# Two rows at a time in narrow blocks, a product in halves, and an earlier request for weights, in one layer of a hybrid encoder

## The chip, the cores and the metric

The kernel runs on one core of a Trainium2 chip. Time is the device time of one execution in microseconds (us); smaller is better. Three runs of the kernel before gave 1913.21, 1913.57 and 1913.68 us, so the median is 1913.57. The engines are TensorE (PE; its weight loads are listed apart as PEld), VectorE (DVE), ScalarE (ACT), GpSimd (POOL) and SyncE (SP), which here issues the DMAs.

## The reference

One inference step of a layer with two parallel branches, for 1024 prompt tokens and 32 sample tokens (1056 in all), width 1024, all in float32:

```
h = RMSNorm(x);  z = h @ w_in          # q/k/v of both branches and their gates
o_a = DiffAttn(h)                      # chunk-causal, two softmax maps per head
o_r = Retention(h)                     # per-frame causal, with decay
x = x + (sigmoid(g_a) * o_a + sigmoid(g_r) * o_r) @ w_o
h = RMSNorm(x)
x = x + (silu(h @ w_ff_gate) * (h @ w_ff_up)) @ w_ff_down
x = x + sigmoid(RMSNorm(x) @ w_ple_gate) * (p @ w_ple)
```

It also returns the new keys, values and retention states. The change touches the line with `w_o`, the second RMSNorm, the first of the gate blocks, and the last line.

## The kernel before, in words

Every float32 operand of a large product is split into two float16 parts, high and low, and a product is three matmuls: high by high, high by low, low by high (`mm3`, lines 474 to 476). Tokens lie along the free axis, features across the 128 partitions, so the width 1024 is eight rows k or m of 128 features.

The program has these stages: the heads of both branches (up to about 1054 us); the w_o products; the gate and up products in 22 feature blocks j (from about 1148 us on); the down products; and the last gate with `w_ple_gate`, up to 1912 us.

**w_o.** The 1056 tokens are cut into four blocks c of 352, 352, 176 and 176 tokens (`WIDTH`). A block has eight products m of 24 matmuls. The task `residual(c)` loads the block's old x into a tile `xf` (line 1546, 1.4 MB for a wide block), and for each m multiplies the product's bank by the weight's scale and adds it to its row of `xf` (line 1553, DVE), writes the row out to DRAM (line 1556), squares it on ACT (line 1561) and adds the square to `acc` on DVE (line 1564). After the eighth, four small matmuls `ss` (line 1572) sum `acc` over the partitions, DVE and POOL make the reciprocal root (lines 1576 to 1582), a matmul with `dg` spreads it over the partitions (line 1587), and DVE scales each row of `xf` with it (line 1591).

**Operands of the gate products.** The gate and up products are done by a Strassen-like scheme over two pairs p of blocks: pair 0 is the two wide blocks, pair 1 the two narrow ones. For seven products per pair and feature block it needs, beside the normed rows, sums and differences of rows (`sums`), into the tiles `xh1` (the same memory as `mixs`) and `tT`. Each operand is split into two float16 parts by `parts16`: a copy on ACT (line 1507) and a subtraction. The subtractions, of `parts16` and of `sums`, go through `either_tt` (line 1501), for which a planner picks DVE or POOL.

**Weights of a gate block.** `load_gu(j)` takes one of two stage buffers `st`, issues a 1 MB load on SP (line 1618), squares it on ACT in two halves (line 1630), adds the two sums on DVE (`wamh`, line 1634), lets a matmul `mt` (line 300) sum them over the partitions, makes the scale on DVE (lines 230, 234, 315, 317), and splits the weights and their combinations (lines 1602, 1605 and 1610) into two float16 parts. The stage buffers also hold w_o's weights: `st_16614` those of the third quarter of its columns and `st_16615` those of the fourth, which are split on ACT (line 459) and DVE (line 461).

**What sets the order.** Up to the down products a planner (`Flow`) writes the order of the instructions of PE, DVE, ACT and POOL out by hand. Each task is a generator that yields the estimated cost of its next step on an engine, a buffer to get or put back, or an event. The planner steps through them in estimated time and always takes the step that can start first, then the lower priority number, then the older task. The estimates are in code: a DVE step of n elements, 0.07 + n / 960 us; an ACT step, 0.1 + n / 1200; a POOL step, 0.15 + 0.0021 n; a DMA, 2.9 us for each MB. An engine then takes its instructions strictly in the written order, and waits where an operand is late. SP issues the DMAs in the order of the program. The stage `stream_bc` names the products in order and adds the tasks beside them.

Of the kernel before, what the change touches and what calls it, by code (L numbers as in the profile page):

```python
# [183 lines left out]
def kernel(  # L184
# [1278 lines left out]
    with ExitStack() as pc:  # L1463
# [18 lines left out]
        with ExitStack() as pw:  # L1482
# [18 lines left out]
                ENG[g].tensor_tensor(out=out, in0=in0, in1=in1, op=op)  # L1501


            def parts16(key, out, src):
                CW = WIDTH[2 * key[0]]
                yield S(CW, 0.05)
                nc.scalar.copy(out[0], src)
                yield from either_tt(CW, out[1], src, out[0], ALU.subtract)
                yield ("set", ("o",) + key)

            def sums(c, k):

                p, CW = c // 2, WIDTH[c]
                xa, xf, t = xfs[c - 1], xfs[c], tT[p]
                a1, a3, b2, b4 = xa[:, k], xa[:, HK + k], xf[:, k], xf[:, HK + k]
                cs = span(c)
                yield ("wait", ("o", p, "x1", k))
                yield from either_tt(CW, a1, b2, a1, ALU.subtract)
                flow.add(parts16((p, "t1", k), (xh1[:, k, 0, cs], xh1[:, k, 1, cs]), a1))

                if not p:
                    yield from either_tt(CW, b2, b4, b2, ALU.subtract)
                    flow.add(parts16((p, "x4", k), (xh1[:, HK + k, 0, cs], xh1[:, HK + k, 1, cs]), b4))
                    flow.add(parts16((p, "t3", k), (t[:, T3, k, 0], t[:, T3, k, 1]), b2))
                    yield ("wait", ("o", p, "x4", k))
                    t2 = b4
                else:
                    yield ("wait", ("o", 0, "t2", k))
                    t2 = xfs[0][:, k, 0:CW]
                yield from either_tt(CW, t2, b4, a1, ALU.subtract)  # L1530
                flow.add(parts16((p, "t2", k), (t[:, T2, k, 0], t[:, T2, k, 1]), t2))
                yield ("wait", ("o", p, "x3", k))
                yield from either_tt(CW, a3, t2, a3, ALU.subtract)
                flow.add(parts16((p, "t4", k), (t[:, T4, k, 0], t[:, T4, k, 1]), a3))
                if p:
                    flow.add(parts16((p, "x4", k), (xh1[:, HK + k, 0, cs], xh1[:, HK + k, 1, cs]), b4))
                    yield from either_tt(CW, b2, b4, b2, ALU.subtract)
                    flow.add(parts16((p, "t3", k), (t[:, T3, k, 0], t[:, T3, k, 1]), b2))

            def residual(c):  # L1540

                p, odd = divmod(c, 2)
                CW = WIDTH[c]
                cs = span(c)
                xf = xc.tile([P, KD, CW], F32, tag="xf%d" % p, name="xf", bufs=2)
                nc.sync.dma_start(out=xf, in_=xT[:, :, cs])
                xfs.append(xf)
                yield ("get", "acc")
                acc = wkb.tile([P, CH], F32, tag="acc", name="acc")[:, 0:CW]
                for m in range(KD):  # L1550
                    yield ("wait", ("wo", c, m))
                    yield V(CW, 1.0, 0.08)
                    nc.vector.scalar_tensor_tensor(out=xf[:, m], in0=banks[c, m], scalar=wos[m // 4][1][m % 4 // 2], in1=xf[:, m],
                                                   op0=ALU.mult, op1=ALU.add)
                    yield ("put", "ps")
                    nc.sync.dma_start(out=x1_d[m, :, cs], in_=xf[:, m])
                    if m:
                        yield ("get", "sq")
                    yield S(CW, 0.05)
                    sq = wkb.tile([P, CH], F32, tag="sq", name="sq")[:, 0:CW] if m else acc  # L1560
                    nc.scalar.activation(sq, xf[:, m], AF.Square)
                    if m:
                        yield V(CW)
                        nc.vector.tensor_tensor(out=acc, in0=acc, in1=sq, op=ALU.add)
                        yield ("put", "sq")
                yield ("get", "ss")
                yield ("delay", 2.0 if c + 1 < NW else 0.5)
                yield M(0.3)
                B = CW // 4
                ps = pss.tile([P, 512], F32, tag="ss", name="ss")  # L1570
                for b in range(4):
                    nc.tensor.matmul(out=ps[0:B, CW + b:CW + b + 1], lhsT=acc[:, b * B:(b + 1) * B], rhs=ones32[:, 0:1],
                                     start=True, stop=True)
# [8 lines left out]
                nc.vector.tensor_tensor(out=dg[0:B].rearrange("p (b c) -> p b c", b=4),  # L1582
                                        in0=id32[0:B, 0:B].unsqueeze(1).broadcast_to([B, 4, B]),
                                        in1=r[0:B].unsqueeze(2).broadcast_to([B, 4, B]), op=ALU.mult)
                yield ("delay", 2.0 if c + 1 < NW else 0.5)
                yield M(0.5)
                nc.tensor.matmul(out=ps[:, 0:CW], lhsT=ones32[0:B], rhs=dg[0:B], start=True, stop=True)
                yield ("put", "acc")
                for k in (0, 4, 1, 5, 2, 6, 3, 7):
                    yield V(CW, 1.0, 0.08)  # L1590
                    nc.vector.scalar_tensor_tensor(out=xf[:, k], in0=xf[:, k], scalar=gS[:, 1, k:k + 1], in1=ps[:, 0:CW],
                                                   op0=ALU.mult, op1=ALU.mult)
                    if not odd:
                        flow.add(parts16((p, "x1" if k < HK else "x3", k % HK), (xh1[:, k, 0, cs], xh1[:, k, 1, cs]), xf[:, k]))
# [201 lines left out]
            def stream_bc():  # L1796
# [1 line left out]
                flow.add(residual(0), 0)  # L1798
                flow.add(residual(1), 0)
                for c in range(NW):  # L1800
                    if c == 1:
                        flow.add(load_gu(0), 2)
                        flow.add(load_gu(1), 2)
                    if c == 3:
                        flow.add(load_gu(2), 2)
                    if c in (1, 2):
                        flow.add(residual(c + 1), 0)
                    for m in range(KD):
                        yield ("get", "ps")
# [125 lines left out]
    with ExitStack() as pe:  # L1935
# [3 lines left out]
        for c in range(NCH):  # L1939
# [5 lines left out]
            for m in range(KD):  # L1945
# [1 line left out]
                    norm2(wk, accs[c + 1], xts[c + 1], c + 1)  # L1947
                ms = slice(m % 4 * P, (m % 4 + 1) * P)
                wt = wps[m // 4][0]
                ps = bank()  # L1950
                for k in range(KD):
                    xt = xts[c][k // 4][:, k % 4]
                    mm3(ps, wt[:, k, 0, ms], wt[:, k, 1, ms], xt[:, 0], xt[:, 1], k == 0, k == KD - 1)
                step()
                th = wk.tile([P, CH], F32, tag="th", name="th")
                nc.scalar.activation(th, ps, AF.Tanh, scale=hdp[:, m // 2:m // 2 + 1])
                nc.vector.scalar_tensor_tensor(out=th, in0=th, scalar=1.0, in1=pws[:, m], op0=ALU.add, op1=ALU.mult)
                yo = wk.tile([P, CH], F32, tag="yo", name="yo", bufs=3)
                nc.vector.scalar_tensor_tensor(out=yo, in0=th, scalar=0.5, in1=x2[:, m, cs], op0=ALU.mult, op1=ALU.add)
                nc.sync.dma_start(out=yT[m, :, cs], in_=yo)  # L1960


# [97 lines left out]
```

## Time and profile before

| | before |
|---|---|
| runs, us | 1913.21, 1913.57, 1913.68 (median 1913.57) |
| profiled execution | 1914.65 us, of it the span 1912.8 us |
| PE busy | 1860.5 us (97%) |
| DVE busy | 1503.2 us (79%) |
| ACT busy | 1091.3 us (57%) |
| POOL busy | 681.9 us (36%) |
| mean granted clock of PE | 0.998 |
| w_o products | 1054.4 to about 1145 us |
| DMA | 146.91 MB, mean 77 GB/s |

Busy time is that of the profiled execution. A matmul of 352 columns is listed with 0.31 us, but the next starts 0.15 us behind it, since matmuls overlap; a product's time is read from the starts. A row of the view of waits says for how long an engine stood still for an operand, and who released it. A row in the timeline ends with such a wait in brackets, where there was one.

### The profile page before, as it was taken

To read this page: it belongs to the slowest core of one execution; us is meant where nothing else is said; L and a number is where in the kernel's file an instruction comes from. 1 tells how busy PE (TensorE), PEld (TensorE's weight loads), DVE (VectorE), ACT (ScalarE), POOL (GpSimd) and SP (SyncE) were. 2 spreads that over 40 slices of the span, in tenths; PEclk is the share of its full clock that TensorE was granted. 3 is DMA by queue.
4 is the path that set the end of the run, shared out by engine and by line. 5 is a ranking of instruction groups with operands and counts; after the bars stand their busy time and mean duration, and the time that the engine had idled before them with its cause. 6 is when DMAs were issued, how large, how long until landed. Compare 5 with 4: busy or idle time off the path is not lost.

```text
span 1912.8 us, 38341 instructions
## 1 busy us (share of the span) xinstructions
PE 1860.5 (97%) x14183; PEld 1217.9 (64%) x14183; DVE 1503.2 (79%) x3955; ACT 1091.3 (57%) x2863; POOL 681.9 (36%) x1162
## 2 busy tenths in 40 slices
PE   7899999999999999999999998999999999999999
PEld 3556565555655566555556685777777776666665
DVE  7888888788787787777887589999999986654364
ACT  7777667677676776767656345655555552101132
POOL 3654444445444544544442067232232300000010
PEclk9999999999999999999999999999999999999999
DMA  5122112122021111211215610222111116112031
GB/s 192 71 72 78 60 32 82 36 57 81 26 68 58 50 64 34 80 59 30 85 34 191 222 65 29 101 83 87 65 59 63 50 53 262 62 61 79 11 133 50
DMA packets 71806, 146.91 MB, mean 77 GB/s; under 512 B 25249, under 2 KB 52001, under 8 KB 63682
## 3 DMA queue, kind: packets, MB, share of 16 engines
q1 hardware_dynamic: 71618, 144.46, 22.5%
q8 instruction: 111, 1.82, 0.4%
q14 instruction: 77, 0.63, 0.1%
HBM read 113.09 MB, written 31.34 MB: 76 GB/s over the span
## 4 chain that ended last, share of the span: by engine, by line
PE 70%; DVE 15%; POOL 6%; ACT 5%; issue 2%; DMA 1%; SPq 0%; POOLq 0%; ACTq 0%; DVEq 0%
PE ps L474 9%; PE ps L475 9%; PE ps L476 9%; PE pj L734 7%; PE pj L735 7%; PE pj L736 7%; PE ps L1478 4%; PE ps L1477 4%; PE ps L1476 4%; DVE nm L885 2%; ACT p L895 2%; DVE w L467 1%; POOL qkr L770 1%; PE sc L875 1%; PE sc L878 1%
## 5 line engine op out<-in xcount | busy, mean ns | idle before, releaser
L734 PE MATMUL pj<-w,xh 128*128 128x512 f16 x1024 | 388.9, 380 | 2.8 <-ACT w L465 2.8
L735 PE MATMUL pj<-w,xh 128*128 128x512 f16 x1024 | 389.0, 380 | 0.6 <-DVE w L467 0.6
L736 PE MATMUL pj<-w,xh 128*128 128x512 f16 x1024 | 389.0, 380 | 0.0
L475 PE MATMUL ps<-mixs,w 128*128 128x352 f16 (+1 forms) x960 | 260.6, 277 | 1.8 <-POOL mixs L1501 1.8
L474 PE MATMUL ps<-mixs,w 128*128 128x352 f16 (+1 forms) x960 | 260.7, 277 | 0.3 <-ACT pws L1354 0.3
L476 PE MATMUL ps<-mixs,w 128*128 128x352 f16 (+1 forms) x960 | 260.5, 277 | 0.0
L474 PEld LDWEIGHTS <-w 128*128 128x128 f16 x1728 | 169.7, 98 | 58.8 <-issue 5.1
L476 PEld LDWEIGHTS <-w 128*128 128x128 f16 x1728 | 169.5, 98 | 56.6 <-issue 5.6
L475 PEld LDWEIGHTS <-w 128*128 128x128 f16 x1728 | 169.5, 98 | 50.1 <-issue 1.3
L736 PEld LDWEIGHTS <-xh 128*128 128x128 f16 x1024 | 100.2, 98 | 122.3 <-issue 1.9
L1610 POOL TENSOR_TENSOR st<-st 128x512 f32<-128x512 f32 x66 | 86.2, 1305 | 250.7 <-DVE w L1605 186.6
L734 PEld LDWEIGHTS <-xh 128*128 128x128 f16 x1024 | 101.4, 99 | 76.7 <-issue 3.7
L735 PEld LDWEIGHTS <-xh 128*128 128x128 f16 x1024 | 100.2, 98 | 74.6 <-issue 3.7
L895 ACT ACTIVATE p<-sc,nb,scs 128x256 f32<-128x256 f32 (+7 forms) x128 | 106.6, 833 | 71.7 <-POOL nb L887 49.1
L475 PE MATMUL ps<-tT,w 128*128 128x352 f16 (+1 forms) x528 | 143.6, 277 | 3.5 <-DVE tT L1501 3.5
L476 PE MATMUL ps<-tT,w 128*128 128x352 f16 (+1 forms) x528 | 143.7, 277 | 0.0
L474 PE MATMUL ps<-tT,w 128*128 128x352 f16 (+1 forms) x528 | 143.6, 277 | 0.0
L1605 DVE SCALAR_TENSOR_TENSOR w<-st,gus,w 128x512 f16<-128x512 f32 x132 | 140.7, 1067 | 0.1
L885 DVE TENSOR_REDUCE nm<-sc 128x2 f32<-128x256 f32 (+6 forms) x112 | 102.9, 918 | 19.5 <-PE sc L878 18.3
L1478 PE MATMUL ps<-a,w 128*128 128x352 f16 x312 | 97.5, 313 | 0.5 <-DVE w L1696 0.5
L1476 PE MATMUL ps<-a,w 128*128 128x352 f16 x312 | 97.5, 313 | 0.0
L1477 PE MATMUL ps<-a,w 128*128 128x352 f16 x312 | 97.5, 312 | 0.0
(432 smaller groups left out, 4874.4 us busy)
## 6 DMA issues: line engine op xcount, KB each, us to landing
st<-in_win_dram SPq DMA_DIRECT2D x30, 1024.0 KB, 4.8
st<-in_wgu_dram SPq DMA_DIRECT2D x22, 1024.0 KB, 4.9
st<-in_wdn_dram SPq DMA_DIRECT2D x16, 704.0 KB, 4.5
out_dram<-kv SPq DMA_DIRECT2D x64, 128.0 KB, 1.7
a_d<-a SPq DMA_DIRECT2D x9, 528.0 KB, 2.6
b<-a_d SPq DMA_DIRECT2D x9, 528.0 KB, 7.1
mixs<-mix_d SPq DMA_DIRECT2D x8, 528.0 KB, 7.0
pw_d<-pws SPq DMA_DIRECT2D x12, 352.0 KB, 5.1
```

The source lines that it names most:

```text
L474: nc.tensor.matmul(out=ps, lhsT=wh, rhs=ah, start=first, stop=False)
L475: nc.tensor.matmul(out=ps, lhsT=wh, rhs=al, start=False, stop=False)
L476: nc.tensor.matmul(out=ps, lhsT=wl, rhs=ah, start=False, stop=last)
L734: nc.tensor.matmul(out=ps, lhsT=xhi, rhs=w[:, k, 0], start=(k == 0), stop=False)
L735: nc.tensor.matmul(out=ps, lhsT=xhi, rhs=w[:, k, 1], start=False, stop=False)
L736: nc.tensor.matmul(out=ps, lhsT=xh[:, k, 1, t0:t0 + P], rhs=w[:, k, 0], start=False, stop=(k == KD - 1))
L885: nc.vector.tensor_reduce(out=nm[0:R, mc], in_=pv, axis=AX.X, op=ALU.max, negate=True)
L895: nc.scalar.activation(pt[0:R, 0:NK], ps[0:R, p0:p0 + NK], AF.Exp, bias=nb[0:R, m:m + 1], scale=sc_ap[0:R], accum_out=Z[0:R, m:m + 1])
L1476: nc.tensor.matmul(out=ps, lhsT=wt[:, 0, j], rhs=a[:, 0, cs], start=(first and j == js[0]), stop=False)
L1477: nc.tensor.matmul(out=ps, lhsT=wt[:, 1, j], rhs=a[:, 0, cs], start=False, stop=False)
L1478: nc.tensor.matmul(out=ps, lhsT=wt[:, 2, j], rhs=a[:, 1, cs], start=False, stop=(last and j == js[-1]))
L1605: nc.vector.scalar_tensor_tensor(out=w[:, i, 1], in0=src, scalar=s, in1=w[:, i, 0], op0=ALU.mult, op1=ALU.subtract)
```

## The change

There are three edits.

First, in the narrow blocks (2 and 3, and pair 1) the rows are handled two at a time (`ROWS = (1, 2)`: one row in pair 0, two in pair 1). One Square, one addition to `acc`, one copy and one subtraction then cover 2 x 176 = 352 elements in a partition. `acc` holds two rows, and the statistics sum both: eight matmuls `ss` in the place of four. The residual itself (one product's bank each), the write to DRAM and the scaling stay by single rows.

Second, `load_gu(0)` is added with the first block of w_o, c = 0; it was added with c = 1. `load_gu(1)` stays at c = 1, `load_gu(2)` at c = 3.

Third, the last product of the program (the last 352 tokens, m = 7) is done as two halves of 176 tokens, each with its own bank, Tanh, two DVE steps and a write.

```diff
+            ROWS = (1, 2)
+
             def parts16(key, out, src):
-                CW = WIDTH[2 * key[0]]
-                yield S(CW, 0.05)
+                p, name, k = key
+                n, CW = ROWS[p], WIDTH[2 * p]
+                yield S(n * CW, 0.05)
                 nc.scalar.copy(out[0], src)
-                yield from either_tt(CW, out[1], src, out[0], ALU.subtract)
-                yield ("set", ("o",) + key)
+                yield from either_tt(n * CW, out[1], src, out[0], ALU.subtract)
+                for j in range(n):
+                    yield ("set", ("o", p, name, k + j))
 
             def sums(c, k):
                 p, CW = c // 2, WIDTH[c]
+                n = ROWS[p]
+                W = n * CW
+                lo, up = slice(k, k + n), slice(HK + k, HK + k + n)
                 xa, xf, t = xfs[c - 1], xfs[c], tT[p]
-                a1, a3, b2, b4 = xa[:, k], xa[:, HK + k], xf[:, k], xf[:, HK + k]
+                a1, a3, b2, b4 = xa[:, lo], xa[:, up], xf[:, lo], xf[:, up]
...
             def residual(c):
...
                     nc.sync.dma_start(out=x1_d[m, :, cs], in_=xf[:, m])
-                    if m:
+                    if m % n + 1 < n:
+                        continue
+                    if m >= n:
                         yield ("get", "sq")
-                    yield S(CW, 0.05)
-                    sq = wkb.tile([P, CH], F32, tag="sq", name="sq")[:, 0:CW] if m else acc
-                    nc.scalar.activation(sq, xf[:, m], AF.Square)
-                    if m:
-                        yield V(CW)
+                    yield S(n * CW, 0.05)
+                    sq = wkb.tile([P, CH], F32, tag="sq", name="sq")[:, 0:n * CW] if m >= n else acc
+                    nc.scalar.activation(sq.rearrange("p (a c) -> p a c", a=n), xf[:, m + 1 - n:m + 1], AF.Square)
+                    if m >= n:
+                        yield V(n * CW)
                         nc.vector.tensor_tensor(out=acc, in0=acc, in1=sq, op=ALU.add)
                         yield ("put", "sq")
...
                 for b in range(4):
-                    nc.tensor.matmul(out=ps[0:B, CW + b:CW + b + 1], lhsT=acc[:, b * B:(b + 1) * B], rhs=ones32[:, 0:1],
-                                     start=True, stop=True)
+                    for j in range(n):
+                        nc.tensor.matmul(out=ps[0:B, CW + b:CW + b + 1], lhsT=acc[:, j * CW + b * B:j * CW + (b + 1) * B],
+                                         rhs=ones32[:, 0:1], start=(j == 0), stop=(j + 1 == n))
...
                 for c in range(NW):
-                    if c == 1:
-                        flow.add(load_gu(0), 2)
-                        flow.add(load_gu(1), 2)
+                    if c < 2:
+                        flow.add(load_gu(c), 2)
                     if c == 3:
                         flow.add(load_gu(2), 2)
...
-                ps = bank()
-                for k in range(KD):
-                    xt = xts[c][k // 4][:, k % 4]
-                    mm3(ps, wt[:, k, 0, ms], wt[:, k, 1, ms], xt[:, 0], xt[:, 1], k == 0, k == KD - 1)
-                step()
...
+                n = 2 if (c, m) == (NCH - 1, KD - 1) else 1
+                for j in range(n):
+                    js = slice(j * CH // n, (j + 1) * CH // n)
+                    os = slice(cs.start + js.start, cs.start + js.stop)
+                    ps = bank()[:, 0:CH // n]
+                    for k in range(KD):
+                        xt = xts[c][k // 4][:, k % 4]
+                        mm3(ps, wt[:, k, 0, ms], wt[:, k, 1, ms], xt[:, 0, js], xt[:, 1, js], k == 0, k == KD - 1)
+                    step()
```

The order of the engines' instructions moves with it. Line numbers of the changed kernel are higher by 4 to 28: its xT load is line 1562, its Square line 1580, its weights' load line 1642 and their squares line 1654.

PE at the start of w_o, behind the third product of block 0 (`mixs` are w_o's operands, `mt` the bank of gate block 0's statistics), before:

```order
L476 MATMUL ps_16904<-mixs_16372,w_15752 128x352
L474 LDWEIGHTS w_15752
L474 MATMUL ps_16935<-mixs_16372,w_15752 128x352
L475 LDWEIGHTS w_15752
L475 MATMUL ps_16935<-mixs_16372,w_15752 128x352
```

and in the changed kernel:

```order
L476 MATMUL ps_16907<-mixs_16372,w_15752 128x352
L300 LDWEIGHTS cst_sb_67
L300 MATMUL mt_16944<-wamh_16935,cst_sb_67 128x1
L474 LDWEIGHTS w_15752
L474 MATMUL ps_16947<-mixs_16372,w_15752 128x352
```

The statistics of gate block 0 stood behind the twelfth product and now stand behind the third.

SP at the same place (`xf` is the block's old x, `pw_d` a write of the stage before, `st` the stage buffer of the gate block's weights), before:

```order
L1362 DMA pw_d_63<-pws_16739 128x2x352
L1546 DMA xf_16828<-in_xT_dram 128x8x352
L1546 DMA xf_16831<-in_xT_dram 128x8x352
L1556 DMA x1_d_64<-xf_16828 128x352 x2
L1546 DMA xf_17082<-in_xT_dram 128x8x176
L1556 DMA x1_d_64<-xf_16828 128x352
L1618 DMA st_17080<-in_wgu_dram 128x2048
```

and in the changed kernel:

```order
L1362 DMA pw_d_63<-pws_16739 128x2x352
L1562 DMA xf_16828<-in_xT_dram 128x8x352
L1562 DMA xf_16831<-in_xT_dram 128x8x352
L1642 DMA st_16834<-in_wgu_dram 128x2048
L1573 DMA x1_d_64<-xf_16828 128x352
L1562 DMA xf_17121<-in_xT_dram 128x8x176
L1562 DMA xf_17399<-in_xT_dram 128x8x176
```

The load of gate block 0's weights moves ahead of the first writes of x and stands right behind the two loads of the wide blocks' old x.

DVE around the last residual of block 3 (`gup`, `gus` and `gud` are the scale of a gate block, `mixs` and `tT` the operands of the gate products), before:

```order
L1553 SCALAR_TENSOR_TENSOR xf<-ps,o1d,xf 128x176
L1591 SCALAR_TENSOR_TENSOR xf<-xf,gS,ss 128x176
L230 TENSOR_SCALAR guc<-mt 128x1
L1501 TENSOR_TENSOR mixs<-xf,mixs 128x176
L234 TENSOR_SCALAR gup_17938<-guc 128x1
L1501 TENSOR_TENSOR mixs<-xf,mixs 128x176
L1564 TENSOR_TENSOR acc<-acc,sq 128x176
L315 RECIPROCAL gus<-gup_17938 128x1
```

and in the changed kernel:

```order
L1570 SCALAR_TENSOR_TENSOR xf<-ps,o1d,xf 128x176
L1611 SCALAR_TENSOR_TENSOR xf<-xf,gS,ss 128x176
L230 TENSOR_SCALAR guc<-mt 128x1
L234 TENSOR_SCALAR gup_17921<-guc 128x1
L315 RECIPROCAL gus<-gup_17921 128x1
L1583 TENSOR_TENSOR acc<-acc,sq 128x352
L317 TENSOR_SCALAR gus<-gus 128x1
L323 TENSOR_SCALAR gud<-gup_17921,gd 128x1
```

The single subtractions into `mixs` leave this place; they follow later as fewer instructions of 128x2x176. Of the 44 subtractions of pair 1, 16 were DVE's and 28 POOL's; of the 22 now, DVE has 7 and POOL 15. Additions to `acc` in blocks 2 and 3 are 6 where they were 14.

More of the change, by code (lines that the diff above doesn't have):

```diff
@@ L1527, in sums @@
                 else:
[L1528 to L1531, printed above, removed]
+                    for j in range(n):
+                        yield ("wait", ("o", 0, "t2", k + j))
+                    t2 = xfs[0][:, lo, 0:CW]
+                yield from either_tt(W, t2, b4, a1, ALU.subtract)
+                flow.add(parts16((p, "t2", k), tr(T2), t2))
                 yield ("wait", ("o", p, "x3", k))
-                yield from either_tt(CW, a3, t2, a3, ALU.subtract)
-                flow.add(parts16((p, "t4", k), (t[:, T4, k, 0], t[:, T4, k, 1]), a3))
+                yield from either_tt(W, a3, t2, a3, ALU.subtract)
+                flow.add(parts16((p, "t4", k), tr(T4), a3))
                 if p:
-                    flow.add(parts16((p, "x4", k), (xh1[:, HK + k, 0, cs], xh1[:, HK + k, 1, cs]), b4))
-                    yield from either_tt(CW, b2, b4, b2, ALU.subtract)
-                    flow.add(parts16((p, "t3", k), (t[:, T3, k, 0], t[:, T3, k, 1]), b2))
+                    flow.add(parts16((p, "x4", k), row(up), b4))
+                    yield from either_tt(W, b2, b4, b2, ALU.subtract)
+                    flow.add(parts16((p, "t3", k), tr(T3), b2))
             def residual(c):
@@ L1548, in residual @@
                 yield ("get", "acc")
-                acc = wkb.tile([P, CH], F32, tag="acc", name="acc")[:, 0:CW]
+                n = ROWS[p]
+                acc = wkb.tile([P, CH], F32, tag="acc", name="acc")[:, 0:n * CW]
                 for m in range(KD):
@@ L1592, in residual @@
                                                    op0=ALU.mult, op1=ALU.mult)
+                    k += 1 - n
+                    if k % n:
+                        continue
                     if not odd:
-                        flow.add(parts16((p, "x1" if k < HK else "x3", k % HK), (xh1[:, k, 0, cs], xh1[:, k, 1, cs]), xf[:, k]))
+                        ks = slice(k, k + n)
+                        flow.add(parts16((p, "x1" if k < HK else "x3", k % HK), (xh1[:, ks, 0, cs], xh1[:, ks, 1, cs]), xf[:, ks]))
                     elif k >= HK:
@@ L1949 @@
                 wt = wps[m // 4][0]
-                ps = bank()
-                for k in range(KD):
-                    xt = xts[c][k // 4][:, k % 4]
-                    mm3(ps, wt[:, k, 0, ms], wt[:, k, 1, ms], xt[:, 0], xt[:, 1], k == 0, k == KD - 1)
-                step()
[L1955 to L1960, printed above, removed]
+                n = 2 if (c, m) == (NCH - 1, KD - 1) else 1
+                for j in range(n):
+                    js = slice(j * CH // n, (j + 1) * CH // n)
[5 more added lines that the diff above has]
+                    step()
+                    th = wk.tile([P, CH], F32, tag="th", name="th")[:, js]
+                    nc.scalar.activation(th, ps, AF.Tanh, scale=hdp[:, m // 2:m // 2 + 1])
+                    nc.vector.scalar_tensor_tensor(out=th, in0=th, scalar=1.0, in1=pws[:, m, js], op0=ALU.add, op1=ALU.mult)
+                    yo = wk.tile([P, CH], F32, tag="yo", name="yo", bufs=3)[:, js]
+                    nc.vector.scalar_tensor_tensor(out=yo, in0=th, scalar=0.5, in1=x2[:, m, os], op0=ALU.mult, op1=ALU.add)
+                    nc.sync.dma_start(out=yT[m, :, os], in_=yo)
 def _tables():
```

14 lines of the change are left out of this document (9 added, 5 removed).

## The prediction

> **What bounds the kernel now.** I read the chip's page first (TensorE, PE, is busy for 97% of the span, as the table above has it), then the waits of PE after the end of the heads. The columns are engine, product and line, the releaser, and then us in total, times, longest. From 1130 to 1245 us:
>
> ```profile
> PE mt L300 <- DVE wamh L1634: 7.3, 5, 3.1
> PE ps L475 <- DVE tT L1501: 3.5, 1, 3.5
> PE ss L1572 <- DVE gus L315: 2.0, 1, 2.0
> PE ps L475 <- POOL mixs L1501: 1.8, 1, 1.8
> PE ss L1587 <- DVE dg L1582: 1.0, 2, 0.6
> ```
>
> The sum is 15.6 us. These are the waits that the merging of rows can shorten. Next the windows: stretch, its length, then busy us of PE, PEld, DVE, ACT and POOL with their counts, the granted clock, DMA share and GB/s.
>
> ```profile
> 1125.00:1150.00 25.00, 21.52 (x259) 19.86 (x258) 24.69 (x48) 14.16 (x38) 20.69 (x21) 0.95 0.11 34
> 1150.00:1175.00 25.00, 21.39 (x143) 13.52 (x142) 24.10 (x51) 14.41 (x36) 21.36 (x25) 0.98 0.15 51
> 1175.00:1200.00 25.00, 17.51 (x178) 15.51 (x176) 24.80 (x50) 12.99 (x31) 15.09 (x16) 0.93 0.11 35
> ```
>
> DVE is busy for 24.1 to 24.8 of 25 us, so in this stretch DVE sets the end, and PE waits for it. Everywhere else in what the change touches PE sets the end: an edit there costs nothing until it makes PE wait.
>
> **Part 1, gate block 0's weights asked for at the first tokens of w_o.** The order of the changed kernel has gu(0)'s statistics matmul `mt` (L300) behind the third w_o product on PE; before it stood behind the twelfth. The question is when that `mt` can run. What stands there before (start, duration, engine):
>
> ```profile
> 1054.83 1.85 SPq L1546 DMA_DIRECT2D xf<-in_xT_dram  x2
> DMA to landing us min/median/max: 6.2/9.6/12.2
> st<-in_wgu_dram SPq DMA_DIRECT2D x3, 1024.0 KB, 7.7
> 1055.01 4.83 DVE L461 SCALAR_TENSOR_TENSOR w<-st,wsk,w 128x256 f16<-128x256 f32 x12
> 1065.14 0.31 PE L474 MATMUL ps<-mixs,w 128*128 128x352 f16 x1
> 1064.57 0.58 DVE L1553 SCALAR_TENSOR_TENSOR xf<-ps,o0d,xf 128x352 f32<-128x352 f32 x1 [4.72 <-DMA xf<-in_xT_dram]
> 1065.19 0.50 ACT L1561 ACTIVATE acc<-xf 128x352 f32<-128x352 f32 x1 [5.66 <-DVE xf L1553]
> 1065.59 1.29 ACT L459 ACTIVATE w<-st,wsk 128x256 f16<-128x256 f32 x3
> 1060.00:1065.00 5.00, 5.00 (x36) 3.26 (x35) 0.43 (x1) 0.00 (x0) 0.00 (x0) 1.00 1.05 372
> L1630 ACT ACTIVATE w<-st x2: 1040/1040/1040, 1087.8 to 1088.9; 128x1024 bf16<-128x1024 f32 x2
> L1630 ACT ACTIVATION_READ_ACCUMULATOR w<-st x2: 187/187/187, 1088.8 to 1089.8; 128x1 f32 x2
> ```
>
> PE reaches the fourth product at 1065.14. The load needs the stage buffer whose last reader is the eighth of the twelve L461 splits (0.40 us apart from 1055.01, so 1058.2), and it then stands in SP's queue behind both 1.4 MB loads of xT, issued at 1054.83. The second of those lands 12.2 us later, at 1067.0. The DMA engines are full meanwhile (share 1.05, 372 GB/s), so the 1 MB behind them needs 1048576 B / 372 GB/s = 2.8 us more: 1069.8, and I take 1070.0 with the completion. Then come two squares (1087.8 to 1090.0 before, 2.2 us), one split that the new order puts between them (1.29 / 3 = 0.43) and the small add and `mt`'s semaphores, an estimate of 0.3 (two steps of the 0.16 that `mt`'s own row below shows): 2.9. PE goes on at 1072.9 instead of 1065.14: **a stall of 7.8 us**. From below: even with the weights there, ACT's first square stands behind Square of the first residual (1065.19, itself held by xT's first load) and a split, so to 1066.0, plus 2.9 = 1068.9: 3.8 us. From above: the load starts only when xT is through and then takes the 7.7 us that the three of its kind take here: 1074.7 and 12.5 us. I take 7.8, which rests on the measured rate.
>
> Nothing covers it: PE is busy throughout there (5.00 of 5.00), and DVE's later crowd starts from w_o's products, so it moves along. Queued behind `mt` on PE is every later w_o product; the residuals wait for those.
>
> After a wait of 3 us PE also runs slow. The trace has one such place:
>
> ```profile
> 1148.03 0.16 PE L300 MATMUL mt<-wamh,cst_sb 128*128 128x1 bf16 x1 [3.07 <-DVE wamh L1634]
> 1148.60 0.50 PE L476 MATMUL ps<-mixs,w 128*128 128x352 f16 x1
> 1148.89 0.50 PE L474 MATMUL ps<-mixs,w 128*128 128x352 f16 x1
> 1151.06 0.31 PE L476 MATMUL ps<-mixs,w 128*128 128x352 f16 x1
> 1151.21 0.31 PE L474 MATMUL ps<-mixs,w 128*128 128x352 f16 x1
> ```
>
> Steps are 0.29 us at first and 0.15 from 1151; between 1148.0 and 1151.0 about ten matmuls lose 0.145 each: 1.45 us. A wait of 7.8 us pays that too, 0.2 to 2.9 by where in such a phase it falls. Loss of part 1: 7.8 + 1.4 = **9.2**. The Trainium skill, "TensorE: Matmul & The Clock Gate", Part 1: The HAM clock gate (the "warmup" mystery), says half the clock after an idle window of about 3.4 us and the whole one after as much work; by that the phase would cost 1.7, and the sum would be 0.3 us higher.
>
> The seven splits and the combinations of gu(0) move from behind its squares at 1090 to behind 1073, into this window:
>
> ```profile
> 1075.00:1090.00 15.00, 15.00 (x102) 9.87 (x101) 3.92 (x7) 4.05 (x8) 0.00 (x0) 1.00 0.54 200
> ```
>
> DVE has 3.92 of 15 us in use there and POOL none, so they cost nothing; without that room they would push block 0's residuals back. Since PE is at 15.00 of 15.00, nothing is won either. gu(1)'s load, squares and `mt` (the 3.1 of the 7.3) keep their place.
>
> The Trainium skill, "DMA: Bandwidth & Descriptors", section "Queues, rings and completion order", says that on each DMA engine the descriptors of SP's ring are consumed in the order of the ring. This speaks against the change, since by it the weights stand behind 2.8 MB of xT; if it did not hold, the stall would be the 3.8 of the lower bound.
>
> **Part 2, two rows at a time.** The instructions of DVE by their forms (count | busy us, mean ns), in and before the crowded stretch:
>
> ```profile
> L1564 DVE TENSOR_TENSOR acc<-acc,sq 128x176 f32<-128x176 f32 x10 | 6.8, 680 | 0.0
> L1564 DVE TENSOR_TENSOR acc<-acc,sq x4: 343/343/343, 1117.6 to 1123.6; 128x176 f32<-128x176 f32 x4
> L1564 DVE TENSOR_TENSOR acc<-acc,sq 128x352 f32<-128x352 f32 x7 | 3.7, 525 | 4.1 <-ACT sq L1561 4.1
> L1501 DVE TENSOR_TENSOR mixs<-xf,mixs 128x176 f16<-128x176 f32 x5 | 3.1, 627 | 0.0
> L1501 DVE TENSOR_TENSOR xf<-xf 128x176 f32<-128x176 f32 x4 | 2.9, 728 | 0.0
> L1501 DVE TENSOR_TENSOR tT<-xf,tT 128x176 f16<-128x176 f32 x5 | 2.3, 484 | 0.0
> L1501 DVE TENSOR_TENSOR mixs<-xf,mixs 128x176 f16<-128x176 f32 x2 | 1.7, 864 | 0.0
> L1501 DVE TENSOR_TENSOR tT<-xf,tT 128x352 f16<-128x352 f32 x8 | 5.5, 703 | 0.0
> L1501 DVE TENSOR_TENSOR xf<-xf 128x352 f32<-128x352 f32 x6 | 5.5, 936 | 0.0
> ```
>
> An add of 176 takes 343 ns alone and 680 while POOL works; one of 352 takes 525 alone and 703 to 936 in company. So the stretching seems to go with the instruction more than with its elements. Adds of squares: 14 become 6, in the crowded part 10 (6.8 us) become 5 of 0.70 to 0.94 (3.5 to 4.7): 2.1 to 3.3 won. Subtractions: 44 become 22; DVE had 16 of them (3.1 + 2.9 + 2.3 + 1.7 = 10.0) and POOL the other 28; in the new order DVE has 7 (4.9 to 6.6) and POOL 15: 3.4 to 5.1 won. Together 5.5 to 8.4. If instead a double row costs by its elements, with only the saving that the quiet prices show (2 × 0.343 - 0.525 = 0.16 for each of 12 pairs, 1.9) and the two row-operations that go over to POOL (2 × 0.625 = 1.3), it is 3.2. I take 6.0, inside the first range and near its lower end. DVE is full there, so PE's waits shrink by as much; with the 3.5 us wait shortened, half of the clock's loss in the last window goes too (0.07 × 25 = 1.75, half is 0.9). Gain **6.9**. The four statistics matmuls (`ss`) of blocks 2 and 3 become eight each, in time in which PE waits for DVE's chain anyway; without that cover they cost at most 8 × 0.16 = 1.3, by the row of `mt`, which is one column wide too.
>
> **Part 3, the last product in halves.** What follows the last matmul, in forms of 352 and, from the gate blocks, 176 elements; then PE's pace in a product 176 wide:
>
> ```profile
> L1956 ACT ACTIVATE th<-ps,hdp 128x352 f32<-128x352 f32 x9 | 5.0, 554 | 25.4 <-PE ps L476 25.4
> L1957 DVE SCALAR_TENSOR_TENSOR th<-th,pws 128x352 f32<-128x352 f32 x9 | 4.7, 526 | 20.4 <-ACT th L1956 20.4
> L1705 ACT ACTIVATE th<-sna,hdg 128x176 f32<-128x176 f32 x3 | 1.3, 426 | 0.0
> L1709 DVE SCALAR_TENSOR_TENSOR th<-th,snu 128x176 f32<-128x176 f32 x1 | 0.3, 341 | 0.0
> 1132.81 0.24 PE L475 MATMUL ps<-mixs,w 128*128 128x176 f16 x1
> 1134.02 0.24 PE L476 MATMUL ps<-mixs,w 128*128 128x176 f16 x1
> ```
>
> The tail gets 554 - 426 = 0.13 and 2 × (526 - 341) = 0.37 shorter: 0.50. PE pays 48 × 1.21 / 16 = 3.63 against 24 × 0.15 = 3.6, nothing. One more DMA is issued before the last; I leave 0.1 for it. Gain **0.4**; 0 if the last write's fixed time sets the end, 0.6 with its half size.
>
> **The sum**: 9.2 - 6.9 - 0.4 = +1.9. On the profiled execution (1914.65, span 1912.8) that is 1916.55; the median of the runs is 1.08 lower, so **1915.5**. Its own range, with 5.5 to 8.4 in the place of the 6.0 and 0.2 to 2.9 in that of the clock's 1.4: 1911.9 to 1917.5.
>
> **Rivals.** *The weights do not wait behind xT*: stall 3.8, sum 3.8 + 1.4 - 6.9 - 0.4 = -2.1, 1911.5. For it: both loads of xT were in flight at once, so a third transfer may be served beside them. Against it: a share of 1.05 leaves no room before 1065, and the load would have to land by then.
>
> *Elements decide* (the other side): DVE stretched by POOL pays a double row nearly double, and the merged chain also releases `ss` and the casts only when two rows are done. Gain 3.2: 9.2 - 3.2 - 0.4 = +5.6, 1919.2. It decides from a gain below 5.0 on, since then the sum passes 3.8. For it: 936 ns against 728 for the same tile. Against it: 680 against 343 for equal elements.
>
> *All of the late waits go*: without the 3.1 for gu(1)'s `mt`, 15.6 - 3.1 = 12.5, with the clock's 1.75 of the last window: 9.2 - 14.25 - 0.4 = -5.4, 1908.1. For it: one chain of DVE feeds all five rows. Against it: DVE would have to win 12.5 of 73.6 us, twice what the counts give.
>
> **How the numbers follow.** Measurements of this kernel tell a change of 0.2% from none, 3.8 us: faster is under 1909.7, slower over 1917.4. Forecast 0.42 (same 0.70, slower 0.20, faster 0.10); first rival 0.17 (same 0.70, faster 0.30); second 0.25 (slower 0.85, same 0.15); third 0.16 (faster 0.75, same 0.25). Summed: faster 0.21, same 0.49, slower 0.30. The range 1908.5 to 1920.5 leaves half of the third rival and the upper edge of the stall's bound outside.
>
> **What would show it.** Right: one wait of `mt` for `wamh` of 7 to 8 us at about 1065, with half-pace matmuls behind it, and the waits after 1150 (plus the shift) down by some 6 us. The first rival shows in that wait being near 4; the second in 352-wide adds above 1.2 us; the third in no waits of L475 and `ss`. I am wrong if `mt` does not wait, or if DVE's windows are no longer full while PE still waits there.

## The result, and the profile after

The changed kernel takes 1921.84 us (median of 5 runs, 1920.49 to 1922.96) where the kernel before takes 1913.32: 1.0044 times as long, 95% interval 1.0033 to 1.0054, so it is 8.5 us slower. Its profiled span is 1920.0 us. The forecast was 1915.5, 1.9 us slower, with a range from 1908.5 to 1920.5. It had the sign right; the size it missed, and the time lies 1.3 us above the range.

PE's waits from 1040 to 1130 us, and from 1130 to 1255 us (engine, product and line, releaser, then us in total, times, longest):

```profile
PE mt L300 <- DVE wamh L1658: 8.7, 1, 8.7
...
PE ps L475 <- DVE mixs L1501: 5.9, 1, 5.9
PE mt L300 <- DVE wamh L1658: 3.5, 2, 2.5
PE ss L1607 <- DVE dg L1602: 2.3, 2, 1.3
PE ss L1592 <- DVE gus L317: 1.0, 1, 1.0
```

The first row is new: `mt` of gate block 0 behind the third w_o product. The late waits are 12.7 us in sum where they were 15.6, and one place, an operand `mixs`, now has nearly half of them.

The start of w_o (start, duration, engine, with the wait in brackets):

```profile
1057.60 2.49 SPq L1642 DMA_DIRECT2D st<-in_wgu_dram  x1
1069.69 1.06 ACT L1654 ACTIVATE w<-st 128x1024 bf16<-128x1024 f32 x1 [4.69 <-DMA st<-in_wgu_dram]
1072.09 0.19 ACT L1654 ACTIVATION_READ_ACCUMULATOR w<-st 128x1 f32 x1
1071.27 1.42 DVE L461 SCALAR_TENSOR_TENSOR w<-st,wsk,w 128x256 f16<-128x256 f32 x1 [5.76 <-ACT w L459]
1072.61 0.57 DVE L1570 SCALAR_TENSOR_TENSOR xf<-ps,o0d,xf 128x352 f32<-128x352 f32 x1
1073.11 0.14 DVE L1658 TENSOR_TENSOR wamh<-gam 128x1 bf16<-128x1 f32 x1
1073.31 0.16 PE L300 MATMUL mt<-wamh,cst_sb 128*128 128x1 bf16 x1 [8.70 <-DVE wamh L1658]
```

The load is issued at 1057.6 and its data arrive at 1069.7. ACT had waited 4.69 us for them, and PE 5.1 by then. `wamh` comes 3.4 us later. ACT's two squares, with a split between them, take 2.6 of this (to 1072.28); a split (1.42 us, where its neighbours take 0.48) and a residual, which stand ahead of `wamh` on DVE, add 0.8.

The windows there and in the crowded stretch (stretch, length, busy us of PE, PEld, DVE, ACT and POOL, granted clock, DMA share, GB/s):

```profile
1065.00:1070.00 5.00, 0.00 (x0) 0.00 (x0) 0.48 (x1) 0.31 (x1) 0.20 (x1) 0.88 1.05 382
1070.00:1075.00 5.00, 1.69 (x7) 0.89 (x7) 3.59 (x8) 3.37 (x8) 2.33 (x2) 0.50 0.92 242
1075.00:1080.00 5.00, 5.00 (x21) 2.71 (x20) 1.92 (x9) 2.25 (x4) 1.26 (x1) 0.60 0.60 226
...
1150.00:1175.00 25.00, 18.13 (x162) 13.12 (x160) 24.00 (x48) 14.99 (x30) 18.64 (x17) 1.00 0.06 20
1175.00:1200.00 25.00, 19.14 (x139) 13.97 (x138) 24.93 (x41) 12.98 (x27) 21.77 (x18) 0.90 0.13 44
1200.00:1225.00 25.00, 25.00 (x240) 20.69 (x239) 24.22 (x58) 14.34 (x31) 9.67 (x7) 0.96 0.24 87
```

DMA is at a share of 1.05 until the weights are there. The clock is 0.50 and 0.60 behind the wait: counted in the timeline, 20 steps of PE are at 0.25 to 0.30 us where the full pace is 0.15, which costs 2.8 us. DVE is still full from 1150 to 1225 us.

One correction to the text ahead of the result: counted by products, `mt` of gate block 0 stood behind the eleventh product before, not the twelfth. No number of the prediction hangs on it.

### The profile page after: what moved, and what is told of

It reads as the page before. It is cut to its first block, busy times and chain, and to the rows that moved or that the text cites. A ratio compares the mean times of both kernels' runs of the same rounds, so it can differ in the third digit from the quotient of the medians.

```text
span 1920.0 us, 38368 instructions
## 1 busy us (share of the span) xinstructions
PE 1862.8 (97%) x14223; PEld 1221.5 (64%) x14223; DVE 1496.6 (78%) x3942; ACT 1088.0 (57%) x2842; POOL 677.1 (35%) x1147
## 4 chain that ended last, share of the span: by engine, by line
PE 69%; DVE 14%; POOL 7%; ACT 5%; issue 3%; DMA 2%; SPq 0%; POOLq 0%; ACTq 0%; DVEq 0%
PE ps L474 9%; PE ps L475 9%; PE ps L476 9%; PE pj L734 7%; PE pj L735 7%; PE pj L736 7%; PE ps L1478 4%; PE ps L1476 4%; PE ps L1477 4%; ACT p L895 2%; DVE nm L885 2%; POOL qkr L770 1%; DVE w L467 1%; PE sc L875 1%; PE t L1072 1%
```

## The experiments

All were measured in the same way as the changed kernel. A difference is against the kernel before on the same chip (medians 1913.8 to 1914.2); the brackets give the 95% interval of the ratio in us.

**One part at a time.** First part 1 on the kernel before, then the changed kernel with part 1 undone, then rows alone and halves alone:

```diff
 e1_only_load: the kernel before, with
-                    if c == 1:
-                        flow.add(load_gu(0), 2)
-                        flow.add(load_gu(1), 2)
+                    if c < 2:
+                        flow.add(load_gu(c), 2)
 e2_rows_halves: the changed kernel with the same lines the other way round
 e3_only_rows: e2 with
-                n = 2 if (c, m) == (NCH - 1, KD - 1) else 1
+                n = 1
 e4_only_halves: e2 with
-            ROWS = (1, 2)
+            ROWS = (1, 1)
```

> The kernel before with part 1 alone (gate block 0's weights asked for with the first w_o block). Theory: the whole loss is one wait of mt for wamh at about 1065 us (8.7 us in the changed kernel) and the half-paced matmuls behind it (granted clock 0.50 and 0.60 in the two windows behind it, about 2.9 us): 1925 us, the waits after 1130 us as before. Rival A, the row merging is worth the forecast 6.9 and something else of part 1 costs more: 1929 or above. Rival B, the row merging is worth nothing: 1922.

> The changed kernel with part 1 undone: rows two at a time and the last product in halves. Theory: 8.5 us slower with part 1, which costs 11.7, leaves a gain of 3.1: 1910.2 us. Rival A (rows worth 6.9): 1906. Rival B (rows worth nothing): 1912.8.

> The kernel before with the rows two at a time alone. Theory: DVE's merged instructions win 9.5 us in the changed kernel's trace, but dg and wamh take 4.1 us longer there beside POOL's longer instructions, and PE's waits fall by about 3: 1910.7 us, with dg at about 2.4 us each. Rival A: 1906.4. Rival B: 1913.3.

> The kernel before with the last product in halves alone. Forecast 0.4 less: 1912.9 us. Rival, the fixed time of the last write sets the end or PE pays for the narrower matmuls: 1913.3 or above.

| | difference, us | interval |
|---|---|---|
| part 1 alone | +11.1 | 8.6 to 13.4 |
| rows and halves | -3.3 | -5.2 to -1.9 |
| rows alone | -2.9 | -4.6 to -1.3 |
| halves alone | -0.7 | -2.5 to 1.0 |

The parts add up: 11.1 - 3.3 = 7.8, against 8.5 for all of them. The theory held, both rivals fell: part 1 does all of the harm, and the rows are worth neither 6.9 nor nothing. The halves' 0.7 cannot be told from zero by times; in the trace the last matmul starts at 1915.85 of a span of 1920.0, and before at 1907.91 of 1912.8, so the tail is 0.74 shorter.

**Why the weights came late.** Two edits of the changed kernel:

```diff
 e5_mt_late: in load_gu, behind the DMA
-                yield ("delay", 2.0)
+                yield ("delay", 2.0 if j else 14.0)
 e6_xT_behind: in load_gu, behind the DMA; and in residual, ahead of xT's load
+                yield ("set", ("ld", j))
...
+                if c == 1:
+                    yield ("wait", ("ld", 0))
```

> The changed kernel, with the weights still asked for at the first tokens, but the squares and mt planned 12 us later: mt stands behind the seventh w_o product (about 1079 us) in the place of the third. Theory: the load itself costs nothing, only mt's place does, so the stall and the slow clock behind it go: 3.3 us below the kernel before, as rows and halves without part 1 (about 1910.9 where before is 1914.2). Rival: the early weights win something once nobody waits for them: 1909 or below. Second rival: the early load itself does harm (to the first residuals, by the full DMA): 1916 or above.

> The changed kernel, with the second block's load of xT issued behind the weights in the place of ahead of them; mt stays behind the third product. Theory (the weights stand behind 2.8 MB of xT): 1.4 MB fewer ahead at 372 GB/s are 3.8 us, so mt waits about 4.9 in the place of 8.7 us and the sum is some 4.5 below the changed kernel, 3.3 above the one before. Rival (the load is late for another reason, the stage buffer or its own transfer): mt waits above 8 us, 7.8 above the kernel before.

With `mt` behind the seventh product the kernel is 3.7 us faster than before (-5.2 to -1.7), as rows and halves without part 1 are. So the early load itself does no harm and no good that the times can tell; the place of `mt` on PE does. With the second block's xT behind the weights the difference is +3.6 (2.1 to 5.6), and PE's waits and the window behind them are

```profile
PE mt L300 <- DVE wamh L1661: 8.7, 4, 4.9
```

```profile
1070.00:1075.00 5.00, 5.00 (x20) 2.61 (x19) 3.05 (x11) 2.49 (x5) 1.26 (x1) 0.53 0.89 264
```

The longest wait is 4.9 us in the place of 8.7, the 3.8 us that 1.4 MB take at 372 GB/s. The landings say the same: the weights land 2.6 us behind the last xT load that was issued ahead of them, in the changed kernel (1067.1 and 1069.7) as in e6 (1063.4 and 1066.0), and 1 MB at 382 GB/s takes 2.7 us. So the load stood behind xT's, and the rival fell. This agrees with the Trainium skill ("DMA: Bandwidth & Descriptors", section "Queues, rings and completion order"), by which each DMA engine takes the descriptors of a ring in the order of the ring.

The kernel's code has a reason why the planner set `mt` so early: `load_gu` yields a price for its load (2.9 us for its 1 MB), but `residual` issues the 1.4 MB loads of xT without a step, so the plan does not have these 2.8 MB ahead of the weights. What order the planner writes with a price for them was not run.

**Which half of the merging wins.** Rows and halves, with the merging in one place only:

```diff
 e7_acc_only
-            ROWS = (1, 2)
+            ROWS, ROWS_A = (1, 1), (1, 2)      # ROWS_A for Square, acc and ss
 e8_ops_only
+            ROWS, ROWS_A = (1, 2), (1, 1)
```

> Rows and halves without part 1, but only the squares, their additions and the statistics go two rows at a time; the copies and subtractions of the operands stay single. Theory: 4.0 of the 9.5 us that DVE wins are the additions', and the wait of 5.9 us for a merged operand (mixs, product 2 of gate block 0's narrow pair) goes back to the two waits of before (1.8 and 3.5); dg stays near 1.2 us. With the halves 0.7: 1.5 to 3 below the kernel before. Rival (the operands carry the gain): 1 or less below.

> Rows and halves without part 1, with only the copies and subtractions of the operands two rows at a time; squares, their additions and the statistics stay by single rows. Theory (the additions' saving ends in dg, which POOL shuts out for 3.4 us where DVE comes early): as good as rows and halves, 3 us below the kernel before, with dg back near 1.2 us. Rival (each half wins its share of what DVE saves, 4.0 of 9.5): 2 below. Second rival (merging the additions does harm): 4 or more below.

The additions alone give -0.8 (-2.5 to 0.8), no more than the halves; the operands alone -2.9 (-4.6 to -1.1). So by the medians the operands carry the gain, though the two intervals overlap, and the theory of the first of the two texts, that the additions have a share of their own, fell. The trace shows one place where time on DVE was lost again. `dg` by its form, in the kernel before, in e7 and in e8:

```profile
L1582 DVE TENSOR_TENSOR dg<-cst_sb,nbr 44x176 f32<-44x176 f32 x2 | 2.4, 1191 | 0.9 <-POOL nbr L1579 0.9
```

```profile
L1602 DVE TENSOR_TENSOR dg<-cst_sb,nbr 44x176 f32<-44x176 f32 x2 | 4.8, 2404 | 1.8 <-POOL nbr L1599 1.8
```

```profile
L1602 DVE TENSOR_TENSOR dg<-cst_sb,nbr 44x176 f32<-44x176 f32 x2 | 2.4, 1188 | 0.9 <-POOL nbr L1599 0.9
```

With the additions merged, `dg` costs 2.4 us more of DVE's time and 0.9 more of waiting; its longest instruction is at 3.4 us in the changed kernel and in every run with merged additions and `dg` on DVE, e11 and e12 excepted. The timeline of rows and halves (e2) shows how, first DVE and then POOL:

```profile
1136.82 3.41 DVE L1602 TENSOR_TENSOR dg<-cst_sb,nbr 44x176 f32<-44x176 f32 x1 [0.91 <-POOL nbr L1599]
...
1135.12 1.66 POOL L1599 TENSOR_TENSOR nbr<-nbv,neghalf 44x4 f32<-44x4 f32 x1 [0.84 <-DVE nbv L1596]
1136.76 1.65 POOL L1501 TENSOR_TENSOR tT<-xf,tT 128x352 f16<-128x352 f32 x2
1138.38 1.65 POOL L1501 TENSOR_TENSOR mixs<-xf,mixs 128x352 f16<-128x352 f32 x2
1140.00 1.38 POOL L1501 TENSOR_TENSOR tT<-xf,tT 128x352 f16<-128x352 f32 x1
```

DVE now comes early, waits for the root `nbr`, and begins `dg` 0.06 us behind POOL's next subtraction. It ends only after four of POOL's in a row (0.82 us each, undisturbed), at 1140.2. In the kernel before, DVE came to `dg` at 1139.62 and was through at 1140.60.

**POOL's share.** Rows and halves, with POOL's merged subtractions issued as two single rows; with none of pair 1's subtractions on POOL; with none at all:

```diff
 e9_pool_single
+                for j in range(out.shape[1]) if g == "G" and len(out.shape) == 3 else ():
+                    nc.gpsimd.tensor_tensor(out=out[:, j], in0=in0[:, j], in1=in1[:, j], op=op)
 e10_pair1_dve, e11_all_dve (there always V)
-                g = yield either(V(n), G(n))
+                g = yield (V(n) if len(out.shape) == 3 and out.shape[1] == 2 else either(V(n), G(n)))
```

> Rows and halves without part 1, in the same order on each engine, but where a merged subtraction falls to POOL it is issued as two single rows; DVE's stay merged. Theory (a DVE instruction that meets POOL's waits for POOL's to end, so POOL's longer ones stretch dg and wamh): dg falls from 2.4 to about 1.2 us, wamh below 0.5 us, and the time is 1 to 2 below rows and halves, 4 to 5 below the kernel before. Rival (POOL's own time decides: 15 instructions more at some 0.2 us each): the time rises by 1 to 3, and dg stays.

> Rows and halves without part 1, with all merged subtractions of the narrow pair on DVE, none on POOL. Theory (a DVE instruction that meets one of POOL's is stretched by about as long as it would take itself): DVE takes on 15 instructions of 0.51 us (7.7 us) and loses some 0.6 us of stretching for each of POOL's 15 (9 us): the time is within 2 of rows and halves, and DVE's adds and splits in that stretch go back to 0.5 and 0.74 us. Rival (POOL's share is simply help): DVE is 7 us later and the time rises by 4 to 7.

> As the run before, with the subtractions of the wide pair on DVE too: POOL does only the weights' combinations and the small roots. Theory: dg, which now lasts 3.4 us at the second narrow statistics while POOL runs four subtractions in a row, falls to about 0.5 us; DVE takes on some 32 of 0.51 us (16 us) and loses 19 us of stretching: within 3 of rows and halves. Rival: DVE is overfilled and the time rises by 8 or more.

Measured: -3.2 (-4.8 to -1.5), -0.1 (-1.9 to 1.5) and +9.6 (7.1 to 11.9). In e9 `dg` stays at 2402 ns and the time does not move (neither of the two forecast times came), so the length of POOL's merged instructions is not what holds it; the four in the row above belong to the wide pair, which e9 leaves alone. In e11, with no subtractions on POOL, the same group reads

```profile
L1602 DVE TENSOR_TENSOR dg<-cst_sb,nbr 44x176 f32<-44x176 f32 x2 | 0.7, 328 | 0.9 <-POOL nbr L1599 0.9
...
L1501 DVE TENSOR_TENSOR xf<-xf 128x352 f32<-128x352 f32 x24 | 12.2, 512 | 0.0
```

and PE's longest waits are

```profile
PE mt L300 <- DVE wamh L1658: 7.2, 1, 7.2
PE ss L1607 <- DVE dg L1602: 4.1, 1, 4.1
```

So it is POOL's subtractions that stretch `dg` and DVE's subtractions. The time did not follow: in e11's order `mt` of gate block 1 stands together with that of block 2 behind all seven products of gate block 0's wide pair, where in e2 it stands ahead of them, and PE waits 7.2 us there and 4.1 for `dg`. The theory for e10 and e11 (DVE's stretching pays for the added instructions) fell. e10 is 3.2 us above rows and halves, less than its rival's 4 to 7, and e11 is 12.9 above, as its rival had it: POOL's share is help.

**The late operand.** Rows and halves, with the first operand of the narrow pair made by single rows, and with the planner's prices raised to what the traces show:

```diff
 e13_t1_single
-                yield from either_tt(W, a1, b2, a1, ALU.subtract)
-                flow.add(parts16((p, "t1", k), row(lo), a1))
+                for j in range(n):
+                    yield from either_tt(CW, a1[:, j], b2[:, j], a1[:, j], ALU.subtract)
+                    flow.add(parts16((p, "t1", k + j), ..., a1[:, j], 1))
 e12_prices
-                g = yield either(V(n), G(n))
+                g = yield either(V(n, 1.0, 0.3), G(n, 0.2))
                 # acc: V(n * CW, 1.0, 0.3); weights: V(HK * P, 1.0, 0.4), G(HK * P, 0.3)
```

> Rows and halves without part 1, but the first difference of the narrow pair (t1, the operand of product 2) is made and split by single rows again; all else stays merged. Theory (a merged operand comes out only when both of its rows are done, and product 2 waits 5.9 us for it, which takes back what DVE wins): that wait falls below 3 us and the time is 1 to 3 below rows and halves, 4 to 6 below the kernel before. Rival (DVE's queue ahead of that operand decides, not its size): the wait stays at 5 to 6 us or moves to the next product, and the time stays within 1 of rows and halves.

> Rows and halves without part 1, with the planner's prices for the crowded DVE and POOL instructions set to what the traces show (0.3 to 0.34 us more on DVE, 0.2 on POOL). Theory (the order puts mt and ss ahead of products that could run, since the plan believes DVE free): the waits of mt and ss fall by 2 to 3 us and the time is 1 to 3 below rows and halves. Rival (DVE is full whatever the order): the wait moves to a later operand and the time stays within 1.

Measured: -1.1 (-3.1 to 0.4) and +4.8 (2.9 to 6.1); both theories fell. PE's waits in e13, and the longest in e12:

```profile
PE mt L300 <- DVE wamh L1659: 6.0, 3, 2.5
PE ps L475 <- DVE tT L1501: 5.4, 1, 5.4
PE ss L1608 <- DVE dg L1603: 1.7, 2, 1.1
```

```profile
PE mt L300 <- DVE wamh L1658: 7.3, 1, 7.3
```

In e13 the 5.9 us went from `mixs` to the next operand, `tT`. That is as the rival had it (what stands ahead in DVE's queue decides, not the size of the merged operand), but the time is 2.2 above rows and halves where the rival had 1. In e12 `mt` of gate block 2 stands behind three products of gate block 0, where in e2 it stands behind five. Its `wamh` comes no earlier (1161.16 us, in e2 1159.85), so PE waits 7.3 us there: the dearer prices did the very thing that they were to undo.

**dg off DVE.** The narrow blocks' `dg` made by four small ACT instructions, in the place of the one on DVE; on rows and halves, on e5, on e8, on e7 and on e4:

```diff
 e14_dg_act, e15_dg_act_early, e16_ops_dg, e17_acc_dg, e18_halves_dg
+                for b in range(4 if p else 0):
+                    nc.scalar.activation(dg[0:B, b * B:(b + 1) * B], id32[0:B, 0:B], AF.Copy, scale=r[0:B, b:b + 1])
```

> Rows and halves without part 1, with the narrow blocks' dg made by four small ACT instructions in the place of the one on DVE; the order of PE and of DVE's other instructions is kept. Theory (DVE stands in dg for 3.4 and 1.4 us, shut out by POOL, and PE's spread of the norm waits for it): DVE has 4.8 us less to do, the wait of the spread (2.3) goes and the time is 2 to 4 below rows and halves, 5 to 7 below the kernel before. Rival (DVE's other instructions take the stretching over): within 1 of rows and halves.

> The changed kernel with mt planned 12 us later and dg of the narrow blocks on ACT: the two edits together. Theory: as the run before within 1 us, since the early weights are worth nothing by themselves. Rival: the stages add something, 1 to 2 lower.

> Halves, merged copies and subtractions, single additions of squares, and dg of the narrow blocks on ACT. Theory (the additions' saving ended in dg): with dg gone from DVE the merged additions are worth about 2, so without them this is 1908.7 + 2, some 3.5 below the kernel before; dg on ACT alone wins less than 1 here (DVE came late to it anyway). Rival (dg on ACT wins 2 by itself): 5 below.

> Halves, merged additions of squares, single copies and subtractions, and dg of the narrow blocks on ACT. Theory: the merged additions, worth 0.1 with dg on DVE, now win about 2: 2.5 to 3 below the kernel before. Rival (the additions are worth nothing either way): 1 to 1.5 below.

> Halves and dg of the narrow blocks on ACT, nothing merged. Theory: dg on DVE came late there and lost little (0.98 and 1.40 us): 0.7 to 1.5 below the kernel before. Rival (dg on ACT wins 2 by itself): 2.7 below.

All with the halves, difference to the kernel before in us:

| merged | dg on DVE | dg on ACT |
|---|---|---|
| nothing | -0.7 | -1.5 (-3.2 to 0.0) |
| additions | -0.8 | -1.5 (-3.3 to 0.2) |
| operands | -2.9 | -4.1 (-5.6 to -2.3) |
| both | -3.3 | -5.4 (-7.5 to -3.4) |

e15 (early weights too, e14 otherwise) is at -4.9 (-6.7 to -2.9), so again the early load adds nothing. e14, at 1908.68 us, is the fastest of all kernels here, 0.28% faster than the kernel before. `dg` on ACT is worth 0.7 to 2.1 by the medians, each within the intervals. For e14 and e18 this is what the theory had; e16 fell between its theory (-3.5) and its rival (-5). But merging the additions wins nothing with `dg` on ACT either where the operands are single (-1.5 against -1.5, where 2 had been expected: e17's rival held), and 1.3 where they are merged, less than the intervals can tell from zero. So the theory that the additions' saving ends in `dg` is not borne out: `dg` took some of it, and taking `dg` away did not bring it back. PE's waits in e14:

```profile
PE ps L475 <- DVE mixs L1501: 5.9, 1, 5.9
PE mt L300 <- DVE wamh L1661: 4.4, 4, 2.3
PE ss L1592 <- DVE gus L317: 1.0, 1, 1.0
PE ss L1610 <- ACT dg L1603: 0.9, 1, 0.9
```

The wait for `mixs` stands at 5.9 us in the changed kernel and in e2, e3, e5, e6, e8, e14, e15 and e16 alike: in all runs that merge the operands and leave their engines, their size and the planner's prices alone. In e9 it is 3.9, and the time is no better.

## Why the prediction was wrong, step by step

**Part 1** was right in mechanism and short in size. Forecast: one wait of `mt` of 7.8 us and 1.4 of slow clock, 9.2. In the trace: 8.7 and 2.8, 11.5; by times, 11.1 with part 1 alone. The landing came out right (PE waited 5.1 us until the data came, I had 1070.0 - 1065.14 = 4.9), in part by luck: I counted the 12.2 us of the second xT load from 1054.83, the start of the first, but the second was issued at 1056.0 and landed at 1068.2, which would have made the wait 1.2 longer; in the changed kernel it landed at 1067.1. The step from the data to PE was set at 2.9 and took 3.6: I counted what stands ahead on ACT, and not the split and the residual that stand ahead of `wamh` on DVE. The clock's 1.4 was taken from one place, and no row stood behind its bounds of 0.2 and 2.9. 20 steps were at half pace here, 17 in e6 (2.4 us) and 10 in e1 (1.4 us): what came in the changed kernel was near the upper bound, and no run showed the lower. The first rival (the weights do not wait behind xT) fell with e6.

**Part 2** was the step that failed: a gain of 6.9 was 2.9. The prices of the instructions were right: the five additions in the crowded stretch take 882 ns each (forecast 700 to 940), and DVE's subtractions went from 22.3 to 15.6 us (the first is the sum of the rows of L1501 from 1125 to 1201 us before), more than forecast. The rows from 1136 to 1212 us of the changed kernel:

```profile
L1501 DVE TENSOR_TENSOR xf<-xf 128x352 f32<-128x352 f32 x9 | 5.5, 631 | 0.0
L1501 DVE TENSOR_TENSOR tT<-xf,tT 128x352 f16<-128x352 f32 x6 | 5.3, 882 | 0.0
L1501 DVE TENSOR_TENSOR mixs<-xf,mixs 128x352 f16<-128x352 f32 x7 | 4.8, 711 | 0.0
L1583 DVE TENSOR_TENSOR acc<-acc,sq 128x352 f32<-128x352 f32 x5 | 4.4, 882 | 0.0
```

What failed is the sentence "DVE is full there, so PE's waits shrink by as much". DVE stayed full (24.0 to 24.9 of 25 us), and more than half of the 9.1 us won on it (2.4 on additions, 6.7 on subtractions) was lost again on DVE itself: `dg` grew by 2.4 us (2.4 to 4.8), `wamh` by 1.7 (six of them, 2.0 to 3.7), twelve splits of weights by 1.1 (10.5 to 11.6) and the 352-wide steps that join gate and up (eight of `th`, four of `a`) by 0.9 each. PE's waits shrank by 2.9 (15.6 to 12.7): `mt` lost 3.8 (7.3 to 3.5), and the others grew by 0.9 in sum. The waits for operands did not shrink, 1.8 and 3.5 became one of 5.9. The other 0.9 of the forecast gain, from the clock, did not come either: the granted clock is 0.97 from 1130 to 1245 us before, and 0.97 from 1140 to 1255 us after.

The rows of e2 show where the 5.9 us arise (ACT's last copy into `mixs` ahead of it, then DVE, then PE):

```profile
1179.11 0.48 ACT L1511 CAST mixs<-xf 128x352 f16<-128x352 f32 x1
1179.16 1.58 DVE L1773 TENSOR_TENSOR snq<-snu,snq 128x352 f32<-128x352 f32 x1
1180.66 1.41 DVE L1629 SCALAR_TENSOR_TENSOR w<-st,gus,w 128x512 f16<-128x512 f32 x1
1181.99 0.51 DVE L1758 TENSOR_TENSOR snu<-snu,ps 128x352 f32<-128x352 f32 x1
1182.42 1.15 DVE L1501 TENSOR_TENSOR tT<-xf,tT 128x352 f16<-128x352 f32 x1
1183.50 1.17 DVE L1501 TENSOR_TENSOR mixs<-xf,mixs 128x352 f16<-128x352 f32 x1
1184.72 0.30 PE L475 MATMUL ps<-mixs,w 128*128 128x176 f16 x1 [5.87 <-DVE mixs L1501]
```

That copy is done by 1179.6, but DVE comes to the subtraction only at 1183.50. Ahead of it in the written order stand two sums of finished products, a split of the next weights and another operand. In the kernel before, POOL made the last row of the same operand. PE came to this product 2.5 us earlier in e2 (1178.85 against 1181.35) and yet went on 1.5 us later (1184.72 against 1183.17). So the place of this one subtraction in DVE's order ends the wait, and not the sum of DVE's work; e5, e8, e14, e15 and e16 have the same instructions there in the same order. The rival "elements decide" gave 3.2 for this gain, near the measured one, but for a reason that did not hold, since the merged instructions were as cheap as forecast. Why DVE's other instructions grew stays open, as does what another place for that subtraction would win: single rows for the first operand moved the wait to the next, taking `dg` away left it at 5.9 us, and no run moved the subtraction alone.

**Part 3** was right in kind, 0.4 against 0.7 in the trace (times cannot tell it from zero).

**The sum** with the measured terms: 8.7 + 2.8 - 2.9 - 0.7 = +7.9, against 8.5 measured. The clock's upper end and the low gain, both in the text, would have made 7.8 + 2.9 - 3.2 - 0.4 = +7.1, 1920.7; the range ended just below, since I let no two of them come together, and then the stall was longer too.

## What to carry to other kernels

A written order is only as good as the arrival times behind it: where an instruction that waits for a load stands in a full engine's queue, count everything ahead of the load on its DMA queue, and everything ahead of each link from the data to that engine. Merging instructions on a full helper engine pays what reaches the engine that sets the end. The helper's busy time does not tell this; find the one instruction that the other engine waits for, see what stands ahead of it in the helper's order, and try the merge alone. A load may be asked for early at no cost if the instruction that needs it keeps its late place (e5).

## What the runs showed of the hardware

A DVE instruction can be shut out by POOL for several of POOL's instructions in a row: `dg`, 328 ns on the mean without POOL's subtractions, took 3.41 us beside four of them. The Trainium skill ("SBUF — State Buffer", section "SBUF: two separate sides") has an exclusive lock between a GpSimd instruction that reads SBUF and a VectorE instruction with two inputs there, and the one who starts first holds it for its whole instruction. The trace agrees on the blocking (POOL began 0.06 us earlier), and here the loser waited for four instructions and not for one.

The slow clock behind a wait of PE is no fixed price: 20 half-pace steps behind 8.7 us (the changed kernel), 10 behind 9.4 us (e1), 17 behind 4.9 us (e6).
